# Dense products of 512 columns issued as two products of 256 columns

## The chip, the cores and the metric

The kernel runs on one core of a Trainium2 chip. The metric is the device time of one execution in microseconds, lower is better. Engines are named as in the profile: PE is TensorE (its products), PEld its loads of the standing operand, DVE is VectorE, ACT ScalarE, POOL GpSimd; SP issues most of the DMAs.

## The reference

Two model blocks run one after the other on 256 tokens of width 1024, all in float32. The first block has two layers of: a SwiGLU feed-forward net, a mixer, a second feed-forward net. The second block has one mixer of another kind and a mixture of 32 experts. What matters here are the dense products of the tokens with streamed weight matrices:

```python
def swiglu(x, w_gate, w_up, w_down):
    return (jax.nn.silu(x @ w_gate) * (x @ w_up)) @ w_down

for i in range(DEPTH):                       # DEPTH = 2, D_MODEL = 1024, D_FF = 2816
    x = x + 0.5 * swiglu(rms_norm(x, ffn1_norm[i]), ffn1_w_gate[i], ffn1_w_up[i], ffn1_w_down[i])
    proj = rms_norm(x, mix_norm[i]) @ w_in[i]
    ...
    x = x + jnp.concatenate([y_ssd, y_att], axis=-1) @ w_out[i]
    x = x + 0.5 * swiglu(rms_norm(x, ffn2_norm[i]), ffn2_w_gate[i], ffn2_w_up[i], ffn2_w_down[i])
```

## The kernel before, in words

A dense product is made in float32r, the form in which PE takes one pass per product, and keeps its accuracy by splitting both factors into a high and a low part: x·w is taken as xh·hi + xh·lo + xl·hi. Tokens are turned once, so that `xh[:, kc, :]` and `xl[:, kc, :]` (or `hh`/`hl` in the down projection, `cath`/`catl` in the mixer's output projection, `oh`/`ol` and `ch`/`cl` in the second mixer) hold 128 rows of the inner dimension (kc counts them) by 256 tokens.

`wstream` (L148) brings the weights: SP issues a DMA of 1 MB into a buffer `raw`, ACT copies it into `hi` (L133), DVE subtracts into `lo` (L134). One `hi`/`lo` pair holds two blocks of 128 rows by 512 columns, and there are three pairs in a ring (`HLB`). After each pair a `tick` lets generators of background work (transposes, the scan, attention, the modulation rows) go one step.

`gemm_x` (L170) uses the weights: for each kc and each of the two halves of the tokens (t) it issues three products into the PSUM bank `ps[t]`, at L178, L179 and L180. The standing operand, which PE must load, is a 128x128 piece of `xh` or `xl`; the moving operand is 512 columns of `hi` or `lo`. Every product has a load of its own: the trace has 9910 products and 9910 loads. `gemm_x` is also called with 256 columns, for the last block of the gate and up projections (2816 = 5·512 + 256; one gate and one up call in each of four feed-forward nets) and in the second mixer, and there with 272 too. `gemm_w` (L183) is the transposed form: weights stand, 256 tokens move (L195 to L197).

The program is built once. Tile, the layer under the kernel, puts each engine's instructions in an order by its own estimate of when operands are ready, so the order can differ a little from that in the code. The mixture of experts, from about 1515 us on, has its own products (L1506, L1539) and does not call `gemm_x`.

Of the kernel before, what the change touches and what calls it, by code (L numbers as in the profile page):

```python
# [49 lines left out]
class Kern:  # L50
# [118 lines left out]

    def gemm_x(self, src, n0, w, xh, xl, k_lo=0, k_hi=None, ps=None):  # L170

        nc = self.nc
        kt = src.shape[0] // P
        ps = ps or [self.t(self.mm, [P, 512], "mm") for _ in range(2)]
        for kc, hi, lo in self.wstream(src, n0, w, k_lo, k_hi):
            for t in range(2):
                sl = slice(t * P, (t + 1) * P)
                nc.tensor.matmul(ps[t][:, :w], xh[:, kc, sl], hi, start=kc == 0, stop=False)  # L178
                nc.tensor.matmul(ps[t][:, :w], xh[:, kc, sl], lo, start=False, stop=False)  # L179
                nc.tensor.matmul(ps[t][:, :w], xl[:, kc, sl], hi, start=False, stop=kc == kt - 1)  # L180
        return ps

    def gemm_w(self, src, n0, w, xh, xl):  # L183
# [1662 lines left out]
```

## Time and profile before

| | us |
|---|---|
| median of 3 runs | 2004.27 (2003.9 to 2008.05) |
| profiled execution | 2003.45 |
| its span, first to last instruction | 2001.6 |
| PE busy | 1946.9 (97%) |
| PEld busy | 1451.0 (72%) |
| DVE busy | 1238.0 (62%) |
| ACT busy | 887.8 (44%) |

A product's shown duration (some 0.39 us at 512 columns, 0.28 us at 256) is that of its whole way through the engine; products follow each other before the one ahead has ended. How many fit into a time is read from the distance between their starts, which the timeline gives.

### The profile page before, as it was taken

How to read it: one execution, taken by the hardware profiler on the slowest of the kernel's cores; microseconds unless marked ns; L12 is line 12 of the kernel's file. 1: busy time of each engine (PE TensorE's matmuls, PEld its weight loads, DVE VectorE, ACT ScalarE, POOL GpSimd, SP SyncE). 2: the span in 40 equal slices, each digit the busy share in tenths (PEclk: the TensorE clock that was granted, in tenths of full speed). 3: DMA queues.
4: the chain of work that ended last, by engine and by line, in shares of the span. 5: the costliest groups of instructions: out<-in, count | busy, mean ns of one | idle time of the engine just before them, and what ended most of it. 6: DMA issues, size and time to landing. Idle time of an engine off the chain costs nothing.

```text
span 2001.6 us, 25699 instructions
## 1 busy us (share of the span) xinstructions
PE 1946.9 (97%) x9910; PEld 1451.0 (72%) x9910; DVE 1238.0 (62%) x2122; ACT 887.8 (44%) x1342; POOL 119.8 (6%) x212
## 2 busy tenths in 40 slices
PE   8999999999999999999999999999998999999996
PEld 6888987888888888897888888888875444444442
DVE  5884797768775876599776555699875122221113
ACT  5444675745444444475665444566643111111101
POOL 1000222100000000014100000100000000000000
PEclk9999999999999999999999999999998999999999
DMA  8885642547876776644345555644486999999996
GB/s 285 277 284 177 195 133 86 179 144 267 270 245 201 261 264 210 198 151 137 106 160 181 175 189 179 195 156 150 160 323 266 421 422 421 420 421 421 421 421 273
DMA packets 193997, 492.61 MB, mean 246 GB/s; under 512 B 11832, under 2 KB 49648, under 8 KB 169296
## 3 DMA queue, kind: packets, MB, share of 16 engines
q1 hardware_dynamic: 187216, 480.89, 66.3%
q0 software_dynamic: 4432, 9.40, 1.5%
q8 instruction: 79, 1.29, 0.3%
q10 hardware_dynamic: 2224, 0.66, 0.2%
q14 instruction: 46, 0.38, 0.1%
HBM read 489.82 MB, written 1.08 MB: 245 GB/s over the span
## 4 chain that ended last, share of the span: by engine, by line
PE 83%; DMA 6%; DVE 6%; ACT 2%; issue 1%; POOL 0%; SPq 0%; DVEq 0%; ACTq 0%
PE mm L178 18%; PE mm L180 18%; PE mm L179 18%; PE mm L1506 9%; DMA raw<-in_w_dram 6%; PE mm L1539 4%; PE tp L206 2%; PE mm L196 2%; PE mm L197 2%; PE mm L195 2%; DVE lo L134 2%; PE tp L1466 1%; PE acc L1558 1%; PE tp L1520 1%; PE ax L720 1%
## 5 line engine op out<-in xcount | busy, mean ns | idle before, releaser
L134 DVE TENSOR_TENSOR lo<-raw,hi 128x1024 fp32r<-128x1024 f32 (+1 forms) x462 | 563.7, 1221 | 279.6 <-ACT hi L133 278.7
L133 ACT ACTIVATE hi<-raw 128x1024 fp32r<-128x1024 f32 (+1 forms) x462 | 486.9, 1055 | 547.1 <-PE mm L180 478.1
L178 PE MATMUL mm<-hi,xh 128*128 128x512 f32 (+1 forms) x1216 | 467.5, 386 | 3.4 <-ACT hi L133 3.3
L179 PE MATMUL mm<-lo,xh 128*128 128x512 f32 (+1 forms) x1216 | 461.7, 380 | 0.2 <-DVE lo L134 0.2
L180 PE MATMUL mm<-hi,xl 128*128 128x512 f32 (+1 forms) x1216 | 460.5, 379 | 0.0
L178 PEld LDWEIGHTS mm<-hi,xh 128*128 128x128 f32 x1216 | 229.3, 189 | 48.1 <-ACT hi L133 4.2
L180 PEld LDWEIGHTS mm<-hi,xl 128*128 128x128 f32 x1216 | 229.5, 189 | 45.5
L179 PEld LDWEIGHTS mm<-lo,xh 128*128 128x128 f32 x1216 | 229.6, 189 | 44.8 <-DVE lo L134 1.6
L1506 PE MATMUL mm<-raw,T 128*64 128x512 f32 x1024 | 239.4, 599 | 1.1 <-DMA raw<-in_w_dram 1.1
L1506 PEld LDWEIGHTS mm<-raw,T 128*64 128x64 f32 x1024 | 72.8, 136 | 123.9 <-issue 112.6
L178 PE MATMUL mm<-hi,hh 128*128 128x512 f32 x352 | 139.3, 396 | 0.0
L180 PE MATMUL mm<-hi,hl 128*128 128x512 f32 x352 | 139.1, 395 | 0.0
L179 PE MATMUL mm<-lo,hh 128*128 128x512 f32 x352 | 138.8, 394 | 0.0
L1539 PE MATMUL mm<-raw,H 128*64 128x512 f32 x512 | 124.3, 597 | 4.1 <-DMA raw<-in_w_dram 4.1
L1539 PEld LDWEIGHTS mm<-raw,H 128*64 128x64 f32 x512 | 42.8, 137 | 70.8 <-issue 49.8
L196 PE MATMUL mm<-xl,hi 128*128 128x256 f32 x320 | 90.0, 282 | 0.3
L195 PE MATMUL mm<-xh,hi 128*128 128x256 f32 x320 | 89.8, 283 | 0.0
L197 PE MATMUL mm<-xh,lo 128*128 128x256 f32 x320 | 89.8, 281 | 0.0
L765 DVE SCALAR_TENSOR_TENSOR macc<-raw,cact,macc 128x512 f32<-128x512 f32 x112 | 83.9, 749 | 3.3 <-DMA raw<-in_w_ada_dram 1.2
L1472 DVE TENSOR_SCALAR T<-tp,cact 128x256 f32<-128x256 f32 x28 | 13.4, 479 | 116.1 <-PE tp L1466 116.1
L180 PEld LDWEIGHTS mm<-hi,hl 128*128 128x128 f32 x352 | 66.2, 188 | 15.2
L179 PEld LDWEIGHTS mm<-lo,hh 128*128 128x128 f32 x352 | 66.2, 188 | 14.9
(430 smaller groups left out, 2584.8 us busy)
## 6 DMA issues: line engine op xcount, KB each, us to landing
raw<-in_w_dram SPq DMA_DIRECT2D x192, 1024.0 KB, 19.8
raw<-in_w_in_dram SPq DMA_DIRECT2D x71, 1024.0 KB, 5.2
raw<-in_ffn_w_up_dram SPq DMA_DIRECT2D x44, 1024.0 KB, 6.9
raw<-in_ffn_w_gate_dram SPq DMA_DIRECT2D x43, 1024.0 KB, 5.2
raw<-in_ffn_w_down_dram SPq DMA_DIRECT2D x40, 1024.0 KB, 5.1
raw<-in_w_ada_dram SPq DMA_DIRECT2D x24, 1024.0 KB, 5.3
raw<-in_w_out_dram SPq DMA_DIRECT2D x20, 1024.0 KB, 5.1
raw<-in_w_ada_f_dram SPq DMA_DIRECT2D x8, 1024.0 KB, 5.3
```

What stands on the lines that cost most here:

```text
L133: nc.scalar.activation(h, r, AF.Copy)
L134: nc.vector.tensor_tensor(l, r, h.bitcast(F32), op=ALU.subtract)
L178: nc.tensor.matmul(ps[t][:, :w], xh[:, kc, sl], hi, start=kc == 0, stop=False)
L179: nc.tensor.matmul(ps[t][:, :w], xh[:, kc, sl], lo, start=False, stop=False)
L180: nc.tensor.matmul(ps[t][:, :w], xl[:, kc, sl], hi, start=False, stop=kc == kt - 1)
L195: nc.tensor.matmul(o, hi[:, sl], xh[:, kc, :], start=kc == 0, stop=False)
L196: nc.tensor.matmul(o, hi[:, sl], xl[:, kc, :], start=False, stop=False)
L197: nc.tensor.matmul(o, lo[:, sl], xh[:, kc, :], start=False, stop=kc == kt - 1)
L206: nc.tensor.transpose(pt[:, j, :], src[:, j * P : (j + 1) * P], self.ident)
L765: last = nc.vector.scalar_tensor_tensor(acc, raw[:, k, :], c, acc, op0=ALU.mult, op1=ALU.add)
L1506: nc.tensor.matmul(pg[s * CAP : (s + 1) * CAP, :], x[:, kc, s, :], w[:, k, :], start=kc == 0, stop=kc == KD - 1,)
L1539: nc.tensor.matmul(pd[nb][q, :], H[:, c, q], w[s][:, k, nb * 512 : (nb + 1) * 512], start=c == 0, stop=c == 3,)
```

## The change

For 512 columns, `gemm_x` issues each product as two: columns 0 to 255 and columns 256 to 511, both with the same standing piece, into the two halves of the same PSUM bank. Only the very first product of a bank (kc = 0, xh·hi, the one that clears it) stays whole. The three lines L178 to L180 become one statement in a loop, at L183 of the changed kernel; all later lines move down by six. In the built program 4496 of the 4656 products of 512 columns become 8992 of 256, and 160 stay whole.

```diff
+        whole = [slice(0, w)]
+        halves = [slice(0, 256), slice(256, 512)] if w == 512 else whole
         for kc, hi, lo in self.wstream(src, n0, w, k_lo, k_hi):
             for t in range(2):
                 sl = slice(t * P, (t + 1) * P)
-                nc.tensor.matmul(ps[t][:, :w], xh[:, kc, sl], hi, start=kc == 0, stop=False)
-                nc.tensor.matmul(ps[t][:, :w], xh[:, kc, sl], lo, start=False, stop=False)
-                nc.tensor.matmul(ps[t][:, :w], xl[:, kc, sl], hi, start=False, stop=kc == kt - 1)
+                for x, y, first, last in ((xh, hi, True, False), (xh, lo, False, False), (xl, hi, False, True)):
+                    for c in halves if kc or not first else whole:
+                        nc.tensor.matmul(
+                            ps[t][:, c], x[:, kc, sl], y[:, c],
+                            start=first and kc == 0, stop=last and kc == kt - 1 and c.stop == w,
+                        )
```

PE's order at the start of the first gate projection of the first layer. The names are the PSUM bank (`mm`), the moving `hi` or `lo` and the standing `xh` or `xl`; the last number is the columns, and x2 means two equal rows in a row. Before:

```order
L178 MATMUL mm_166<-hi_171,xh_93 128x512
L178 MATMUL mm_167<-hi_171,xh_93 128x512
L179 MATMUL mm_166<-lo_172,xh_93 128x512
L180 MATMUL mm_166<-hi_171,xl_94 128x512
L179 MATMUL mm_167<-lo_172,xh_93 128x512
L180 MATMUL mm_167<-hi_171,xl_94 128x512
L178 MATMUL mm_166<-hi_171,xh_93 128x512
```

After, the same place:

```order
L183 MATMUL mm_166<-hi_171,xh_93 128x512
L183 MATMUL mm_167<-hi_171,xh_93 128x512
L183 MATMUL mm_166<-lo_172,xh_93 128x256 x2
L183 MATMUL mm_166<-hi_171,xl_94 128x256 x2
L183 MATMUL mm_167<-lo_172,xh_93 128x256 x2
L183 MATMUL mm_167<-hi_171,xl_94 128x256 x2
L183 MATMUL mm_166<-hi_171,xh_93 128x256 x2
```

Each product after the two clearing ones became a pair; the sequence of banks and operands is the same.

DVE's order in the second column block of the same feed-forward net, where background steps (`macc`, L763 and L765 before, L769 and L771 after) run between the subtractions that make `lo`. Before:

```order
L763 TENSOR_SCALAR macc_497<-raw_498,cact_328 128x512
L134 TENSOR_TENSOR lo_424<-raw_421,hi_423 128x1024
L210 TENSOR_TENSOR hl_165<-tp_374,hh_164 128x4x128
L765 SCALAR_TENSOR_TENSOR macc_497<-raw_498,cact_328,macc_497 128x512 x2
L134 TENSOR_TENSOR lo_440<-raw_421,hi_439 128x1024
```

After:

```order
L769 TENSOR_SCALAR macc_681<-raw_682,cact_420 128x512
L771 SCALAR_TENSOR_TENSOR macc_681<-raw_682,cact_420,macc_681 128x512 x2
L134 TENSOR_TENSOR lo_562<-raw_559,hi_561 128x1024
L216 TENSOR_TENSOR hl_165<-tp_488,hh_164 128x4x128
L771 SCALAR_TENSOR_TENSOR macc_681<-raw_682,cact_420,macc_681 128x512
```

Two background steps moved ahead of one subtraction. SP's queue of DMAs is the same in both programs.

## Rows read from the trace of the kernel before

**Rows 1.** Busy time by stage: span, PE, PEld, DVE, ACT, POOL (instructions), clock, DMA

```profile
0.00:200.00 200.00, 191.41 (x888) 156.60 (x889) 135.87 (x165) 94.44 (x117) 14.40 (x31) 1.00 0.75 256
200.00:450.00 250.00, 243.69 (x1390) 208.08 (x1389) 199.35 (x445) 158.32 (x285) 42.34 (x70) 1.00 0.46 147
...
1275.00:1515.00 240.00, 234.83 (x1408) 204.78 (x1406) 207.17 (x363) 139.79 (x204) 11.16 (x19) 0.99 0.57 192
1515.00:2001.60 486.60, 457.44 (x2132) 200.39 (x2131) 116.21 (x255) 70.59 (x136) 0.00 (x0) 0.98 0.96 398
```

**Rows 2.** Waits: PE's longest, and who waits longest of all (total, times, longest)

```profile
PE tp L206 <- DVE xg L232: 7.1, 1, 7.1
PE tp L665 <- DVE q L657: 5.7, 4, 2.6
...
ACT hi L133 <- PE mm L180: 478.1, 291, 5.4
```

**Rows 3.** PE timeline, 512 columns, xh/xl standing: start, duration, engine, line, operands

```profile
456.06 0.39 PE L179 MATMUL mm<-lo,xh 128*128 128x512 f32 x1
...
477.99 0.40 PE L180 MATMUL mm<-hi,xl 128*128 128x512 f32 x1
```

**Rows 4.** PE timeline, 256 columns in `gemm_x`, first eight kc of gate

```profile
131.72 0.28 PE L178 MATMUL mm<-hi,xh 128*128 128x256 f32 x1
...
134.33 0.28 PE L180 MATMUL mm<-hi,xl 128*128 128x256 f32 x1
...
135.34 0.28 PE L178 MATMUL mm<-hi,xh 128*128 128x256 f32 x1
...
138.05 0.29 PE L180 MATMUL mm<-hi,xl 128*128 128x256 f32 x1
```

**Rows 5.** PE timeline, 256 columns in `gemm_w`

```profile
1303.52 0.39 PE L195 MATMUL mm<-xh,hi 128*128 128x256 f32 x1
...
1326.12 0.28 PE L197 MATMUL mm<-xh,lo 128*128 128x256 f32 x1
```

**Rows 6.** PE timeline, 512 columns: `hh`/`hl` of the last net, then `cath`/`catl`

```profile
1247.52 0.39 PE L178 MATMUL mm<-hi,hh 128*128 128x512 f32 x1
...
1275.22 0.39 PE L180 MATMUL mm<-hi,hl 128*128 128x512 f32 x1
...
432.57 0.40 PE L178 MATMUL mm<-hi,cath 128*128 128x512 f32 x1
...
441.73 0.40 PE L179 MATMUL mm<-lo,cath 128*128 128x512 f32 x1
```

**Rows 7.** Products of tile `mm` in these stretches: span, PE (products), clock, DMA, GB/s

```profile
456.05:478.05 22.00, 22.00 (x96) 1.00 0.84 289
131.70:134.40 2.70, 2.70 (x25) 1.00 0.73 247
135.30:138.10 2.80, 2.76 (x24) 1.00 0.24 91
138.70:144.00 5.30, 5.30 (x48) 1.00 0.78 273
1303.50:1326.20 22.70, 22.68 (x192) 1.00 0.45 143
1247.50:1275.30 27.80, 27.80 (x124) 1.00 0.58 189
432.55:441.80 9.25, 9.25 (x42) 1.00 0.44 125
```

**Rows 8.** PE timeline: a stream of 256 columns just after transposes

```profile
1205.17 0.28 PE L179 MATMUL mm<-lo,xh 128*128 128x256 f32 x1
...
1205.52 0.28 PE L179 MATMUL mm<-lo,xh 128*128 128x256 f32 x1
...
1207.68 0.28 PE L180 MATMUL mm<-hi,xl 128*128 128x256 f32 x1
```

**Rows 9.** DMA queue that brings instructions: packets, MB, share of 16 engines

```profile
q8 instruction: 79, 1.29, 0.3%
```

## The prediction

> **What bounds the kernel now.** I read the table of stages first. Up to 1515 us PE is busy 97 to 98% of each stage while DVE stands at 54 to 86%, ACT at 46 to 64% and the DMA engines at up to 0.75 [rows 1]. Only after 1515 us do the DMA engines fill (0.96), and `gemm_x` is not called there. The list of waits says the same from the other side: PE's own longest waits before the experts are 7.1 and 5.7 us in total, whereas ACT waits 478.1 us for PE to give back a `hi` buffer [rows 2]. So the weights are ready ahead of PE, and in the first 1515 us the time is the sum of the distances between the starts of PE's products. A change to those distances goes to the end nearly undiminished: PE is busy 191.41 of the first 200 us and 243.69 of the next 250, and some of the rest is start-up.
>
> The durations shown for products (0.39 us at 512 columns) do not serve, since products overlap; the starts do. With `xh`/`xl` standing, 95 products of 512 columns (96 in the window's count, one of which began before it) lie from 456.06 to 477.99 us: 21.93 / 94 = 233.3 ns each [rows 3, 7]. The clock in that window is 1.00 of full, so 2.4 GHz, the upper level, and 512 columns at it are 213.3 ns; about 20 ns per product are something else. The question is how much of those 20 ns a product of 256 columns has.
>
> **What 256 columns cost here.** The trace holds the changed form almost exactly: `gemm_x` with 256 columns, same standing tiles, same ring, own load for each product. In the first eight kc of a gate projection 24 products lie from 131.72 to 134.33 us, 2.61 / 23 = 113.5 ns each. The next 24, in the same call, lie from 135.34 to 138.05 us: 2.71 / 23 = 117.8 ns [rows 4, 7]. These are two rhythms rather than a spread: a stream keeps one of them until something interrupts it. Just after transposes it can start at 117 ns (1205.17 to 1205.52 us, 3 steps) and then fall to 113.7 (1205.52 to 1207.68, 19 steps) [rows 8]. `gemm_w`, with the operands in exchanged roles, holds the slow rhythm for 192 products: 22.60 / 191 = 118.3 ns [rows 5, 7].
>
> The four feed-forward nets have 16 such groups of 24. Going through the timeline I count 13 at the fast rhythm and 3 at the slow one (the second group of the gate projection, in three nets), each time right behind a 512-column product of the modulation rows. The mean is (13 · 113.5 + 3 · 117.8) / 16 = 114.3 ns, and a pair is 228.6 ns.
>
> Products of 512 columns have rhythms too. With `hh`/`hl` of the last feed-forward net standing there are 123 products, so 122 steps, in 27.70 us: 227.0 ns. With `cath`/`catl` 40 steps take 9.16 us: 229.0 ns [rows 6, 7]. So 227.0, twice the fast rhythm of 256, is reached by whole products also; a split there has nothing to gain.
>
> **The change part by part.**
> - *4496 products of 512 become pairs; 160 stay whole.* By place: 260 pairs in the last net's down projection at 227.0 now, 376 with `cath`/`catl` at 229.0, and the other 3860 at 233.3 (I take the second mixer's 504 with these).
>  - 3860 · (228.6 − 233.3) = −18.1 us
>  - 260 · (228.6 − 227.0) = +0.4 us
>  - 376 · (228.6 − 229.0) = −0.2 us
>  - sum −17.9 us
> - *Bounds of the pair.* All at the fast rhythm: 227.0, so −24.3, 0 and −0.8, together −25 us. All at the rhythm of `gemm_w`: 236.6, so 3860 · 3.3 + 260 · 9.6 + 376 · 7.6 = 12.7 + 2.5 + 2.9 = +18 us. I take the value between by the groups of the same function, because operands, addresses and the banks' order are those.
> - *4496 loads more.* Their cost is in the distances above, since each product there has its load; they are not added again.
> - *Orders that moved.* In the feed-forward nets two background steps go ahead of one `lo` on DVE. DVE has 64 of 200 us free, and the time in which ACT waits for PE to give a buffer back shows how far the two run ahead [rows 1, 2]. I cost that at nothing; if the lead were gone, a `lo` late by one step would cost PE less than a microsecond at each of some tens of places. In the mixers some scan and attention products stand up to 12 places, and once 70, elsewhere among the dense ones; this can cost or spare a few microseconds, and I take nothing.
> - *What is late next.* Nothing: with PE 2% quicker DVE in the densest stage goes from 86% to 88%, DMA from 0.75 to 0.77.
>
> PE's share puts the gain at −17.9 · 0.98 = −17.5 us. Against the profiled execution, 2003.45 us, this gives 1986; against the median of the runs, which is 0.8 us above it, 1987.
>
> **A rule that speaks against it.** First the rows: 2 · 113.5 = 227.0 is the same as the fast whole product, so splitting has no fixed price at that rhythm, and against 233.3 it gains [rows 3, 4, 6]. The Trainium skill ("TensorE: Matmul & The Clock Gate", section "Back-to-back issue gap") puts a warm product at its columns divided by 2.4 GHz plus about 2.5 ns. By that every split adds 2.5 ns, and the sum would be 4496 · 2.5 = +11 us, 2015 us. The rows at 113.5 disagree with its constant (113.5 − 106.7 = 6.8 ns, and 20 ns at 512, so the extra is not fixed per product), and those at 117.8 give a price of the same sign and size, by the rival next.
>
> **The rivals.**
> - *The stream falls into the slow rhythm and stays.* My conjecture for the rhythms is that loads and the reading of columns get in each other's way; each half needs a new standing tile after 113 ns instead of 233, so it would happen twice as often. For it: `gemm_w` sits there for 22 us at a stretch and three of the groups do too. Against: after a product of 512 columns of the same call the stream went to 113.5 at once, and in the new order every call begins with two whole products. At 117.8 a pair costs 235.6: 3860 · 2.3 + 260 · 8.6 + 376 · 6.6 = 8.9 + 2.2 + 2.5 = +13.6 us, 2018 us. It decides as soon as three quarters of the pairs are slow: (233.3 − 227.0) / (235.6 − 227.0) = 0.73.
> - *A mixture near that point.* Between 60 and 85% slow: within some 4 us of 2004.
> - *The mixers keep their part.* DVE has 199 of 250 us there and 207 of 240 in the second mixer [rows 1]; if waits on it eat the 1112 pairs of the mixers and the 504 of the second, −17.9 shrinks to the 2620 pairs of the nets at 233.3, −12.3 + 0.4, so 1992 us. Against: PE is at 97% there too.
> - *Instructions come too late.* 79 packets of 1.29 MB bring the program [rows 9]. An estimate: the 19820 products and loads of PE account for nearly all, so 8992 more would be 36 more packets, spaced 15 us in place of 28. If each held PE a microsecond: +36 − 17.5 = +18 us, 2022. Against: PE ran 192 products of 256 in 22.6 us without a gap [rows 5].
> - *The pairs are merged back, or the load is shared.* Excluded by the order: 8992 products stand there, and a product has its load.
>
> **How the numbers follow.** What three runs can tell from no change is about 0.2%, 4 us. Chances: forecast 0.54, with its own range 1977 to 1996; the mixers keep their part 0.08; mixture 0.14; slow rhythm 0.21; instructions 0.03. The first two are faster; the mixture is the most of "same". The range goes from 1977 (all fast, −25, with a little of the reordering) to 2014 (nine tenths of the way from the forecast to the all-slow case); beyond it lie the rest of that rival and the instructions, not 2 in 10. Faster 0.62, same 0.14, slower 0.24.
>
> **What would show it.** In the profile of the changed kernel the starts of the halves in a feed-forward net tell at once: 113.5 apart for the forecast, 118 for the rival. The stage from 456 us should be 2% shorter, the last net's down projection unchanged, and ACT's waits for PE still in the hundreds of microseconds. I am wrong if halves stand at 118 in most groups, if PE gets gaps that begin at an instruction packet, or if waits on `lo` grow from nothing to several microseconds.

## The result, and the profile after

The changed kernel takes 2020.03 us (median of 4 runs, 2016.63 to 2020.58) against 2004.09 us before: ratio 1.0072, 95% interval 1.0059 to 1.0084. It is slower by 16 us, where 1987 us and a gain were forecast. The span of the profiled execution grew from 2001.6 to 2018.8 us.

First the page of the changed kernel: its span, the busy time by engine, the queue that brings instructions, and the first line of the chain of work that ended last.

```profile
span 2018.8 us, 34684 instructions
PE 1954.8 (97%) x14406; PEld 1666.1 (83%) x14406; DVE 1242.8 (62%) x2122; ACT 884.3 (44%) x1340; POOL 117.6 (6%) x212
...
q8 instruction: 115, 1.88, 0.4%
...
PE 76%; DVE 12%; DMA 7%; ACT 3%; issue 2%; SPq 0%; DVEq 0%; ACTq 0%
```

The same line of the kernel before:

```profile
PE 83%; DMA 6%; DVE 6%; ACT 2%; issue 1%; POOL 0%; SPq 0%; DVEq 0%; ACTq 0%
```

PE is 97% busy as before, with 4496 products more, and only 7.9 us more of busy time. The span grew by 17.2 us, so more than half of the loss is time in which PE does not work. The chain says where to look: DVE has 12% of it, before 6%. The instruction queue has 36 packets more [rows 9].

The same stretches as in [rows 1] (span, then PE, PEld, DVE, ACT and POOL busy with their instructions, granted clock, DMA share, GB/s):

```profile
0.00:200.00 200.00, 190.13 (x1574) 187.59 (x1575) 135.85 (x165) 94.15 (x117) 13.97 (x31) 1.00 0.75 256
200.00:450.00 250.00, 240.40 (x1900) 231.47 (x1898) 196.93 (x440) 151.35 (x276) 40.81 (x70) 0.98 0.44 140
1275.00:1515.00 240.00, 233.84 (x1895) 228.70 (x1894) 202.89 (x353) 138.84 (x195) 11.19 (x19) 0.99 0.57 193
```

In the first 200 us (mostly a feed-forward net) DVE and the DMA engines have done the same work to within 0.02 us and in the same share: this net won next to nothing. In the first mixer PE lost 3.3 us of busy time, DVE did less work, and the granted clock fell from 1.00 to 0.98. The waits, to set beside [rows 2] (total, times, longest):

```profile
ACT hi L133 <- PE mm L183: 485.5, 293, 5.7
...
PE tp L671 <- DVE q L663: 10.6, 8, 3.6
```

The weights are still ready ahead of PE (ACT waits 485.5 us). But PE's wait for `q`, normalised by DVE before PE turns it, grew from 5.7 us at 4 places to 10.6 at 8.

A stage runs from its first dense product to the first of the next stage. Worked out so from the starts in the traces, the difference to before in us, with two of the experiments below beside it:

| stages | after | halves, order of before | whole, order of after |
|---|---|---|---|
| gate and up projections, four nets | −1.3 | −0.4 | −0.7 |
| down projections, first three nets | −2.0 | −0.4 | +0.7 |
| down projection, last net | +3.4 | +3.2 | +0.3 |
| first two mixers, projections with `xh`/`xl` | +8.6 | −0.5 | +9.3 |
| their `gemm_w` stages | +2.2 | +0.3 | +0.9 |
| their output projections (`cath`/`catl`) | +2.5 | +1.3 | +1.0 |
| second block's mixer | +3.3 | +1.1 | +2.3 |
| start, experts | +0.4 | +0.6 | −0.7 |
| span | +17.2 | +5.1 | +13.1 |

So two questions: why the mixers lost 8.6 us and more, and why the nets, with some 20 ns of apparent reserve per product, won 3.3 us where some 12 were forecast. The second is read from the timeline of the changed kernel in the second net's first projection (start, duration, line, operands; x2 are two halves in a row):

```profile
471.64 0.39 PE L183 MATMUL mm<-hi,xl 128*128 128x256 f32 x2
...
472.32 0.39 PE L183 MATMUL mm<-hi,xl 128*128 128x256 f32 x2
472.55 0.39 PE L183 MATMUL mm<-hi,xh 128*128 128x512 f32 x1
472.78 0.40 PE L183 MATMUL mm<-lo,xh 128*128 128x256 f32 x2
473.01 0.40 PE L183 MATMUL mm<-hi,xl 128*128 128x256 f32 x2
473.25 0.40 PE L183 MATMUL mm<-hi,xh 128*128 128x512 f32 x1
473.48 0.40 PE L183 MATMUL mm<-lo,xh 128*128 128x256 f32 x2
...
474.66 0.40 PE L183 MATMUL mm<-hi,xh 128*128 128x256 f32 x2
```

From 471.64 to 472.55 stand 8 halves, 0.91 / 8 = 113.8 ns: the fast rhythm. At 472.55 the whole product that clears the first bank comes, four halves, and at 473.25 the one that clears the second. From then on 10 halves lie from 473.48 to 474.66: 118 ns, and the stream keeps that for its remaining 13 us. This answers [rows 3] and [rows 8]: both rhythms are there, and in these stages 59 to 72% of the halves are slow, so a pair takes 232 to 233 ns on the mean against 233.3.

The streams of [rows 6] got slower outright. First and last lines of the last net's `hh`/`hl`, then of `cath`/`catl`:

```profile
1259.69 0.36 PE L183 MATMUL mm<-lo,hh 128*128 128x256 f32 x1
...
1289.53 0.40 PE L183 MATMUL mm<-hi,hl 128*128 128x256 f32 x2
...
450.96 0.48 PE L183 MATMUL mm<-lo,cath 128*128 128x256 f32 x2
...
460.47 0.40 PE L183 MATMUL mm<-hi,catl 128*128 128x256 f32 x2
```

Here, 248 steps in 29.84 us are 120.3 ns, 240.6 a pair, where whole products took 227.0. With `cath`/`catl`, 80 steps in 9.51 us are 118.9, the first two of them longer.

### The profile page after: what moved, and what is told of

Read it like the earlier page. It is cut to its first block, busy times and chain, and to the rows that moved or that the text cites. A ratio compares the mean times of both kernels' runs of the same rounds, so it can differ in the third digit from the quotient of the medians.

```text
span 2018.8 us, 34684 instructions
## 1 busy us (share of the span) xinstructions
PE 1954.8 (97%) x14406; PEld 1666.1 (83%) x14406; DVE 1242.8 (62%) x2122; ACT 884.3 (44%) x1340; POOL 117.6 (6%) x212
## 4 chain that ended last, share of the span: by engine, by line
PE 76%; DVE 12%; DMA 7%; ACT 3%; issue 2%; SPq 0%; DVEq 0%; ACTq 0%
PE mm L183 48%; PE mm L1512 8%; DMA raw<-in_w_dram 7%; PE mm L1545 4%; DVE lo L134 3%; PE tp L212 2%; PE mm L202 2%; PE mm L203 2%; PE mm L201 2%; PE tp L1472 1%; PE acc L1564 1%; ACT hi L133 1%; DVE cacc L1170 1%; PE tp L1526 1%; PE ax L691 1%
## 5 line engine op out<-in xcount | busy, mean ns | idle before, releaser
L133 ACT ACTIVATE hi<-raw 128x1024 fp32r<-128x1024 f32 (+1 forms) x462 | 487.2, 1056 | 543.7 <-PE mm L183 485.5
L183 PE MATMUL mm<-hi,xh 128*128 128x256 f32 (+1 forms) x2112 | 470.5, 292 | 3.3 <-ACT hi L133 3.3
L183 PE MATMUL mm<-lo,xh 128*128 128x256 f32 x2240 | 464.7, 282 | 0.1
L183 PE MATMUL mm<-hi,xl 128*128 128x256 f32 x2240 | 463.6, 281 | 0.0
L183 PEld LDWEIGHTS mm<-lo,xh 128*128 128x128 f32 x2240 | 360.5, 190 | 6.8 <-DVE lo L134 0.8
L183 PEld LDWEIGHTS mm<-hi,xl 128*128 128x128 f32 x2240 | 350.3, 189 | 0.1
L183 PEld LDWEIGHTS mm<-hi,xh 128*128 128x128 f32 x2112 | 337.7, 190 | 6.1 <-ACT hi L133 3.5
L183 PE MATMUL mm<-hi,hh 128*128 128x256 f32 (+1 forms) x688 | 140.7, 283 | 0.0
L183 PE MATMUL mm<-lo,hh 128*128 128x256 f32 x704 | 139.5, 280 | 0.0
L183 PE MATMUL mm<-hi,hl 128*128 128x256 f32 x704 | 139.1, 279 | 0.0
L183 PEld LDWEIGHTS mm<-lo,hh 128*128 128x128 f32 x704 | 108.5, 189 | 0.7
L183 PEld LDWEIGHTS mm<-hi,hl 128*128 128x128 f32 x704 | 107.5, 189 | 0.0
L183 PEld LDWEIGHTS mm<-hi,hh 128*128 128x128 f32 x688 | 105.9, 189 | 0.2
L771 DVE SCALAR_TENSOR_TENSOR macc<-raw,cact,macc 128x512 f32<-128x512 f32 x112 | 84.0, 750 | 4.0 <-DMA raw<-in_w_ada_dram 1.3
```

The costliest lines, as they stand in the source:

```text
L133: nc.scalar.activation(h, r, AF.Copy)
L183: nc.tensor.matmul(ps[t][:, c], x[:, kc, sl], y[:, c], start=first and kc == 0, stop=last and kc == kt - 1 and c.stop == w,)
L771: last = nc.vector.scalar_tensor_tensor(acc, raw[:, k, :], c, acc, op0=ALU.mult, op1=ALU.add)
```

## The experiments

Four theories. A: most of the loss is the order into which Tile put the mixers' work, and the halves themselves cost little. B: the slow rhythm costs it, in all stages. C: the distance from one product to the next depends on where standing and moving tile lie to each other in a partition of SBUF, modulo 256 bytes. By their addresses, the built programs have `hi` and `lo` at 0xA0; `xh`/`xl` and the first three nets' `hh`/`hl` at 0xE0 (233.3 ns whole); the last net's `hh`/`hl` at 0xA0 (227.0); `cath`/`catl` at 0x60 (229 to 230). D: the place plays no part.

**Halves in the order of before.** The program is recorded twice, first with whole products; then, with halves, each engine's order is fixed to the first one's, a pair standing where its product stood.

```diff
+    for SPLIT in (False, True):
+        nc, arrays, args, out = fresh()
+        pin = trace(args, out, nc, pin)
```

> All products split as in the changed kernel, but every engine's instructions held in the order of the kernel before. Theory A (most of the loss comes from the changed order in the mixers: waits, and the clock's drops that follow them; the pairs themselves cost about 3 us in sum): about 2007 us. Theory B (the loss is the slow rhythm of the halves, spread over all 4496 pairs): as the changed kernel, about 2020 us.

Measured 2008.25 us, ratio 1.0019 (1.0009 to 1.0028): A, not B. The halves themselves cost about 4 us, of which the last down projection has 3.2 and the output projections 1.3; the mixers' projections with `xh` are back at −0.5 (table above).

**Whole products in the order of after.** The same with `(True, False)`.

> Products of 512 columns left whole, but every engine's instructions held in the order of the changed kernel. Theory A: 2014 to 2017 us, with the waits of PE for DVE in the mixers that the changed kernel shows. Theory B: about 2004 us.

Measured 2017.32 us, ratio 1.0062 (1.0045 to 1.0079). Without one half in it, the new order costs 13 us. The two parts, +4 and +13, add up to the change's +16 within a microsecond or so. The projections of the first two mixers have 9.3 us of it. Its timeline in the first mixer (in square brackets the idle time before, and what ended it):

```profile
298.09 1.05 PE L570 MATMUL ax<-X,wk 128*128 128x128 f32 x8
302.84 1.12 PE L676 MATMUL tp<-csq,q 128*128 128x128 f32 x4 [3.69 <-DVE q L668]
303.61 0.78 PE L187 MATMUL mm<-hi,xh 128*128 128x512 f32 x1
304.18 0.63 PE L187 MATMUL mm<-lo,xh 128*128 128x512 f32 x1
```

These turns in the kernel before, then in the changed kernel:

```profile
304.11 0.66 PE L665 MATMUL tp<-csq,q 128*128 128x128 f32 x4 [2.33 <-DVE q L657]
...
304.57 1.11 PE L671 MATMUL tp<-csq,q 128*128 128x128 f32 x4 [3.65 <-DVE q L663]
```

Before, ten dense products stood between the `ax` products and these turns, and PE waited there for 2.33 us. In the new order 12 dense products stand behind the turns instead: PE comes earlier, waits 3.65 or 3.69 us, and after the wait the products run at about 427 ns in place of 233. So of the 9.3 us in these projections, 4.9 are longer waits for `q` (10.6 us in all in place of 5.7), and some 2.7 the spell at 427 ns in the first mixer (an estimate: 5.9 us from the turns to its end, which by 233 in place of 427 ns would be 3.2). The granted clock is the third number from the end in a row of the table of windows. The stretch from 303 to 310 us in the kernel before:

```profile
303.00:310.00 7.00, 5.89 (x36) 5.18 (x37) 6.66 (x10) 3.19 (x5) 2.34 (x4) 1.00 0.28 85
```

In the changed kernel:

```profile
303.00:310.00 7.00, 5.43 (x26) 5.43 (x27) 4.72 (x8) 0.69 (x1) 0.55 (x1) 0.51 0.39 143
```

And in this one:

```profile
303.00:310.00 7.00, 7.00 (x24) 5.82 (x25) 3.48 (x6) 1.68 (x3) 0.00 (x0) 0.59 0.16 63
```

1.00 is 2.4 GHz; 0.51 is the lower level, 1.2 GHz, nearly throughout. Around its wait of 2.33 us the kernel before kept the upper level; around 3.65 and 3.69 us the other two lost it.

**The turns later.** The order of after, whole products, but in each of the first two mixers 12 dense products go ahead of the four turns again; nothing else moves.

```diff
+            for spot in (960, 3216):
+                k = at[spot]
...
+                pe[k - 4 : k + 12] = pe[k : k + 12] + pe[k - 4 : k]
```

> Whole products in the changed kernel's order, but at one place in each of the first two mixers TensorE's four turns of q (tp<-csq,q) stand behind the 12 dense products that followed them, as they did before the change. If the order costs time because these turns stand where VectorE has not finished q (waits of 3.97 us, 12 and 8 products at half clock behind them): the two waits fall to under 1.5 us, the products behind run at 233 ns, and the time comes down by 5 to 9 us from 2017.3, to 2008 to 2012. Rival, VectorE is late on the whole and PE then waits at the next thing it makes: 2015 to 2018.

Measured 2011.02 us, ratio 1.0032 (1.002 to 1.0045): 6.3 us back by two places. The turns of the first mixer, then the waits for `q` in all:

```profile
305.25 0.66 PE L676 MATMUL tp<-csq,q 128*128 128x128 f32 x4 [0.90 <-DVE q L668]
...
PE tp L676 <- DVE q L668: 5.0, 8, 1.1
```

And the same stretch in the table of windows:

```profile
303.00:310.00 7.00, 5.77 (x35) 4.65 (x34) 6.90 (x11) 2.85 (x5) 3.53 (x5) 1.00 0.47 150
```

At this place the wait fell from 3.69 to 0.90 us, by 2.79: that is the time of 12 products at 233 ns. The longest wait fell from 3.7 to 1.1 us, the total from 10.6 to 5.0, and the clock stays at 1.00. The rival that PE would wait just as long at the next thing is out. The other 7 us of the order lie in smaller pieces (in this profile 2.0 in the first mixer's `gemm_w` stage, 2.0 in the two mixers' projections, 1.6 in the second block's mixer) that no run takes apart. The first of these is in part a spell of the lower clock, 0.50 from 252.5 to 255.8 us, behind a wait of 1.94 us for ACT; with the same wait and no spell, the run with the whole order of after lost 0.7 there.

**Where the rhythm comes from: the two clearing products together.** Halves, order of before, but both whole products of a call first.

```diff
+            if kc == 0:
+                todo.sort(key=lambda p: p[1] > 0)
```

> Halves in the order of before, but the two whole clearing products of a tile pair stand next to each other, ahead of the ten others of their block (x kc 0), so that no whole product stands between two halves. If a whole product between halves is what starts the slow rhythm (118 ns in place of 113): the halves with xh and xl of a feed-forward net fall from 116 to 114 ns or less, and the time from 2008.3 to 1992 to 2000. Rival, the slow rhythm starts anyhow (at the turns of h, at a bank's change): 116 ns and 2007 to 2010.

Measured 1996.03 us, ratio 0.9956 (0.994 to 0.9973): 12 us less than with the same halves in the order above, faster than before. The timeline of the second net's first projection:

```profile
461.57 0.40 PE L189 MATMUL mm<-hi,xh 128*128 128x256 f32 x2
461.81 0.40 PE L189 MATMUL mm<-lo,xh 128*128 128x256 f32 x2
462.04 0.40 PE L189 MATMUL mm<-hi,xl 128*128 128x256 f32 x2
462.28 0.63 PE L189 MATMUL mm<-hi,xh 128*128 128x512 f32 x2
462.75 0.39 PE L189 MATMUL mm<-lo,xh 128*128 128x256 f32 x2
...
463.66 0.39 PE L189 MATMUL mm<-hi,xh 128*128 128x256 f32 x2
```

Ahead of the two whole products the stream is slow (461.57 to 462.04: 4 steps, 117.5 ns); behind them it is fast (462.75 to 463.66: 8 steps, 113.8). Over the nets' gate and up projections the halves' mean is 114.0 to 115.3 ns, which misses the expected 114 or less: slow stretches still begin elsewhere, as this one did, behind turns. Against the kernel before, the gate and up projections are 6.6 us shorter and the first three down projections 4.4. A whole product alone among halves is thus one thing that starts the slow rhythm, and it does so each time: in these projections, all 39 streams of six or more halves right behind a single whole product are slow in the changed kernel, and all 38 behind two in a row are fast here. (One stream behind two in a row, in the first call of the run with halves in the order of before, is slow all the same.) Why two in a row end it was not tried.

**The place of `xh` and `xl`.** Whole products, order of before; the pool of `xh`/`xl` is made ahead of three others, so that they lie at 0xA0 modulo 256, like `hi`/`lo`.

```diff
+            xp = dense.enter_context(tc.tile_pool(name="xT", bufs=1))
+            self.xh = self.t(xp, [P, KD, 256], "xh", F32R)
+            self.xl = self.t(xp, [P, KD, 256], "xl", F32R)
             self.dc = dc = dense.enter_context(tc.tile_pool(reuse_waits="tile", name="dense", bufs=1))
```

> The kernel before with the standing tiles xh and xl put at another place of SBUF: 87456 and 95648 in place of 106464 and 114656, so that they stand at the same place within 256 bytes as the weights hi and lo (which hh and hl of the last feed-forward net did, at 227.0 ns a product). Same order of instructions. Theory C (the distance between products is set by where standing and moving tile lie to each other): products with xh or xl at 227 ns, 3080 of them times 6.3 ns less, about 1985 us. Theory D (the place plays no part): 2004 us.

Measured 1991.44 us, ratio 0.9928 (0.9911 to 0.9944). The stream of [rows 3], the same 95 products:

```profile
454.27 0.39 PE L187 MATMUL mm<-lo,xh 128*128 128x512 f32 x1
...
475.61 0.39 PE L187 MATMUL mm<-hi,xl 128*128 128x512 f32 x1
```

21.34 / 94 = 227.0 ns in place of 233.3. D is out. In `gemm_w` the same move shifts the moving tile, `xh`/`xl`, while the weights stand where they stood. The stream of [rows 5]:

```profile
1295.35 0.39 PE L206 MATMUL mm<-xh,hi 128*128 128x256 f32 x1
...
1318.37 0.28 PE L208 MATMUL mm<-xh,lo 128*128 128x256 f32 x1
```

23.02 / 191 = 120.5 ns in place of 118.3, so the place of the moving tile counts too, as C says. That only the distance between the two counts is not shown: no run moved both alike. The time fell by less than the expected 19 us because the 528 products of 256 columns in `gemm_x` went the other way, from 114.5 to 119.6 ns on the mean, the 960 in `gemm_w` from 117.5 to 119.8, and the mixers' 768 came only to 229. Together that is 2.7 + 2.2 + 1.5 = 6.4 us, the whole difference to 1985.

**Halves with `xh` and `xl` there.** The same move with halves, order of before.

```diff
-    for SPLIT in (False,):
+    for SPLIT in (False, True):
```

> All products split, order of the kernel before, xh and xl moved as in the run before this one. Theory C: halves with xh or xl take the 119.9 ns that halves with hh or hl of the last feed-forward net take in the changed kernel, 240 a pair against 232 now, so some 20 to 25 us above the split kernel in the old order: about 2030 us. Theory D: as the split kernel in the old order, about 2007 us.

Measured 2025.84 us, ratio 1.0104 (1.0088 to 1.0121), a little under the expected 2030. The same stream:

```profile
460.53 0.36 PE L187 MATMUL mm<-hi,xh 128*128 128x256 f32 x1
...
483.36 0.40 PE L187 MATMUL mm<-hi,xl 128*128 128x256 f32 x2
```

In it 190 halves' widths (four of the products are whole) take 22.83 us: 120.2 ns. At the place where whole products are quickest, halves are slowest, in every stage and without a fast rhythm. That is also the last net's `hh`/`hl` in the changed kernel.

**Other places for `hh` and `hl`.** Whole products, order of before, `xh`/`xl` moved, and a pad ahead of `hh` in the first three nets: 0x60, 0x20, 0xA0.

```diff
+            n = self.nets = getattr(self, "nets", 0) + 1
+            if SPLIT and n < 4:
+                self.t(pool, [P, 16 * (2, 1, 3)[n - 1]], "pad")
```

> Whole products, order of before, xh and xl moved; hh and hl of the first three nets lie at three other places: 0x60, 0x20 and 0xA0 modulo 256 bytes (before: 0xE0 in all three, the last at 0xA0). If the distance goes by the place modulo 256: about 230 ns at 0x60 (as cath there), about 233 at 0x20 (as ol there), 227 at 0xA0 and 227 in the last net. Rival, what counts is something else that the move of x changed: the three nets run alike, at 233.

One run, 1991.55 us. First and last of 123 products in each of the three nets:

```profile
176.60 0.39 PE L187 MATMUL mm<-hi,hh 128*128 128x512 f32 x1
...
204.54 0.39 PE L187 MATMUL mm<-hi,hl 128*128 128x512 f32 x1
...
611.97 0.39 PE L187 MATMUL mm<-hi,hh 128*128 128x512 f32 x1
...
640.43 0.39 PE L187 MATMUL mm<-hi,hl 128*128 128x512 f32 x1
...
802.51 0.39 PE L187 MATMUL mm<-hi,hh 128*128 128x512 f32 x1
...
830.20 0.39 PE L187 MATMUL mm<-hi,hl 128*128 128x512 f32 x1
```

27.94 / 122 = 229.0 ns at 0x60, 28.46 / 122 = 233.3 at 0x20, 27.69 / 122 = 227.0 at 0xA0, by nothing but up to 192 bytes of padding: without it, in the run with `xh` and `xl` moved alone, all three nets have 233.3. The rival is out.

**All standing tiles moved.** Whole products, order of before; `xh`/`xl`, all `hh`/`hl`, `cath`/`catl` at 0xA0 (the second block's stay).

```diff
+            if SPLIT and n < 4:
+                self.t(pool, [P, 48], "pad")
...
+            if SPLIT:
+                self.t(pool, [P, 16], "gap")
```

> Whole products, order of before; xh and xl moved as in the run with them alone (1991.4), and now hh, hl and cath, catl too, so that all of them lie where hi and lo lie modulo 256 bytes. If the place of the standing tile against the moving one sets the distance: the 792 products of hh and hl that ran at 233 run at 227 (4.8 us) and 384 of cath at 227 in place of 230 (1.1 us), 1985 to 1986. Rival, only the streams of x depend on it: 1991.

Measured 1986.98 us, ratio 0.9908 (0.9891 to 0.9924), a microsecond above the expectation. The first three down projections run at 227.1 ns and are 4.5 us shorter than before. The products with `cath`/`catl` went only to 229 on the mean, so place is not the whole of their distance. This is the fastest version: 17 us under the kernel before, 33 under the changed one.

## Why the prediction was wrong

The forecast missed by 33 us. Two steps of it failed: the price of a pair makes up some 21 us (−17.5 forecast, +4 in the order of before), the moved orders some 13 (taken as nothing).

- *What bounds the kernel.* Right for the nets: PE's distances, weights ahead of it, and the experts unchanged. (The first stage of [rows 1] has PE at 96%, not at 97 or 98; nothing rests on it.) In the mixers PE's waits for DVE belong to it too.
- *The pair at 228.6 ns.* This step failed most. The mechanism, two rhythms kept until an interruption, was right, and so was the price under its premise: with both clearing products first, the nets' pairs take 228 to 231, and the nets' gate and up and first three down projections are 11.0 us shorter, where −12.3 was forecast. The premise failed. "In the new order every call begins with two whole products" was read from the first call, and holds in 1 of 80: in 78 the second whole product stands four halves later, and the slow rhythm starts. The fast group of [rows 4] that stood for it came behind a long run of whole products, in a call of its own. The sign that the prediction had named, halves at 118 in most groups, is there: 59 to 72% in the gate and up projections. So −12.3 became −3.3 in the changed kernel, −0.9 in the order of before.
- *The last down projection, +0.4, and `cath`, −0.2.* Wrong in size: +3.4 and +2.5 (the latter with 1.0 of order in it). I carried 113.5 and 117.8 over from `xh`, "because operands, addresses and the banks' order are those"; for these tiles the addresses are others, halves there run at 117 to 120 ns, and the quick 227.0 of whole products is a property of the place, not of a rhythm that halves share.
- *"Orders that moved ... I take nothing".* Wrong by about 13 us. For the feed-forward nets it held (the whole products in the new order changed the nets' three rows of the table by less than a microsecond each). For the mixers I had read that scan and attention products move up to 12 places and did not ask what each of them would wait for. The wait stood in [rows 2]: turns of `q` on DVE, 5.7 us. With DVE's order as it is in the changed kernel, turns that come 12 products earlier on PE wait 2.79 us longer (0.90 against 3.69). Against the kernel before, with ten products in between, the wait grew by 1.3 us only; DVE's order changed there as well. In both profiles of the new order the lower clock came with the longer wait. The claim that DVE's free time is a lead for PE was true of `lo` and not of `q`.
- *Bounds and rivals.* In the old order the halves alone gave +4 us: the mixture, at its upper edge, not the slow rhythm throughout. The total of 2020 lies by the slow rival's 2018 by accident: 13 us of it is order. *The mixers keep their part* had the right place, waits for DVE, but only a lost gain of some 6 us where 13 were lost outright. *Instructions come too late* is out: 36 packets more as estimated, and no gap in the streams shown (the 79 packets before are 25 us apart on the mean, not 28).
- *The rule of the Trainium skill* ("TensorE: Matmul & The Clock Gate", section "Back-to-back issue gap"), about 2.5 ns for every product more, would give +11 us for any split, by estimate. The section states it for an isolated product; for a stream of loads and products it gives about 131 ns at 512 columns, and the streams of 512 columns in `gemm_x` here have 227.0 to 233.3. The same halves gave +4, −8 and +21.5 us with another first product order or another place of `xh`, so no fixed price per product describes them.
- *What is late next: "Nothing".* Wrong for the same reason as the order.

## What to carry to other kernels

When a change alters the number of instructions, compare the scheduler's order in every stage, and price each moved instruction by its producer: time by which it moves ahead of work that another engine sets comes back as a wait, and a lower clock may come with it. Before splitting products to save some nanoseconds each, measure the same stream at another address; here moving the standing tiles was worth 17 us, and the best split 8. A premise about a stream's start has to be counted over all calls, not read from the first.

## What the runs showed of the hardware that I had not expected

- The distance of float32r products with their own load depends on where standing and moving tile lie modulo 256 bytes. With the moving tile at 0xA0, whole products of 512 columns: 227.0 ns with the standing tile at 0xA0, 229.0 at 0x60, 233.3 at 0x20 and 0xE0. Halves turn it round: 113.5 or 118 at 0xE0, 117 to 118 on the mean at 0x60, 120 at 0xA0. (Counted in 512 bytes, the last net's `hh` lies at 0x0A0 and the moved `xh` at 0x1A0, and both have 227.0.)
- At 0xE0 halves have two stable rhythms, and one whole product can put a stream from one into the other for 13 us.
- Around waits of 3.65 and 3.69 us on PE in the first mixer the granted clock fell to its lower level (1.2 GHz) until 5 to 6 us behind them; around one of 2.33 us in the same work, and of 0.90 us with the turns later, it did not. The length of the last wait does not settle it: the kernel before has such a spell, 0.51 from 934.8 to 938.3 us, behind 2.63 us in the second mixer, and the changed one a further one, 0.50 from 251.8 to 255.2 us, behind 1.93 us. In the run with `xh` and `xl` moved, the turns of the first mixer lost the upper level behind 2.36 us:

```profile
301.74 0.66 PE L676 MATMUL tp<-csq,q 128*128 128x128 f32 x4 [2.36 <-DVE q L668]
...
302.30:305.70 3.40, 3.40 (x12) 2.84 (x12) 2.69 (x4) 2.13 (x3) 0.00 (x0) 0.50 0.00 0
```

So it is not shown that the longer wait alone brings the lower clock.
